# Two-part values product, a later load of x and queued weight splits in a hybrid attention layer

## The chip, the cores and the metric

One core of a Trainium2 chip runs one launch of the kernel. The metric is the device time of that launch in microseconds (us). Five engines work in parallel, each through its own queue in order: PE (TensorE, matrix products), DVE (VectorE), ACT (ScalarE), POOL (GpSimd) and SP (SyncE, which here only issues DMAs). PEld is PE's loading of the stationary operand, which overlaps the products.

## The reference

One decoder layer over 256 tokens of width 1024. One projection feeds three token mixers; their outputs are gated, merged and normalised, and a feed-forward part with a second gate follows.

```python
proj = x @ w_in[i]
o_a = dsa_mixer(...)      # 6 heads, one k and v for all, the 64 best keys by an index
o_b = dilated_mixer(...)  # 3 groups x 4 slots, merged over the groups: 4 value products
o_c = moba_mixer(...)     # 6 heads, 256 keys
gates = jax.nn.sigmoid(x @ w_gate[i]).reshape(bsz, s_len, N_BRANCH, D_MODEL)
merged = (gates[:, :, 0] * (o_a @ w_br_a[i]) + gates[:, :, 1] * (o_b @ w_br_b[i])
          + gates[:, :, 2] * (o_c @ w_br_c[i]))
x = layer_norm(ALPHA * x + merged @ w_out[i], ln1_g[i], ln1_b[i])
h = jnp.square(jax.nn.relu(x @ w_up[i])) @ w_down[i]
ple = jax.nn.sigmoid(x @ w_ple_gate[i]) * (p[i] @ w_ple[i])
x = layer_norm(ALPHA * x + h + ple, ln2_g[i], ln2_b[i])
```

## The kernel before

Every float32 product is made from two-part operands: a high part `hi`, the value rounded to the type F32R, and a low part `lo`, what the rounding left, and three products hi·hi, hi·lo and lo·hi (`prod`, L131 to L134). A product of 128x128 stationary values with a moving block of 256 or 512 columns is called a pass here.

**Weights.** `Weights` (L50 to L90) streams the weights in units of up to 128x1024. For each unit SP loads it into one of five `raw` buffers (L71), ACT makes `hi` (L75) and DVE, or DVE and POOL together for the first 58 units, makes `lo` (L79), into five pairs of buffers. The next load into a `raw` buffer waits until its `lo` is made. `get` asks for the splits four units ahead; whatever stands in `W.after` at that moment is an instruction behind which the split is queued on that instruction's engine. Every engine works in the order in which a scheduler put the program at build time.

**Heads (to about 193 us).** For each of 16 heads, `head` or `slots` (L338 to L373) turns logits into probabilities P, laid out as 384 columns: 128 for the queries 0 to 127 (keys 0 to 127) and 256 for the queries 128 to 255 (all keys). `attend` (L307) transposes P in three 128x128 blocks into a PSUM bank (L312 to L314), makes `hi` (ACT, L315) and `lo` (DVE, L316) in 512-wide tiles `pth` and `ptl`, whose first 128 columns were set to zero once by POOL (L194), and makes four passes of 256 columns (L319 to L322) with the stationary `V[:, j, vh]`. The 128 columns of `V` hold the high part of a value head in the first 64 and the low part in the last 64, so the output's rows 0 to 63 and 64 to 127 must be added: ACT copies the lower half to `ov` (L324) and DVE adds it to the upper one (L325). There is one PSUM bank for the transposes (b3) and one for the outputs (b4). `pair_out` splits a pair of heads into `op` (ACT L328, DVE L329). Between the heads PE is filled with passes of the gate products ("g") and of the branch products ("c", `fill` L233).

**Merges (about 196 to 206 us).** Four calls of `merge` (L559) each make 18 passes over `op[:, 0..2]`, gate them on DVE (L568, L569) and split two tiles `m` (ACT L572, DVE L573). `outp` (L577) multiplies these tiles with the eight units of `w_out` into four banks b0 to b3, 96 passes of 512 columns: units 0 to 3 by `step`, units 4 to 7, whose parts lie in `hT`, by `finish` (L545), which ends first the two banks of the tokens 0 to 127 (b = 0: b0 and b1), then those of b = 1 (b3 and b2).

**First layer norm (about 226 to 241 us).** `ln1` (L621) adds ALPHA·x, which the ACT queue loads into `PL` (L596, 1 MB), takes statistics (L605 to L613, one of them on POOL, L612), norms with the rows `rows1` (L593, 1 MB, ACT queue), transposes the result (L632) and splits it into `x1` (ACT L634, DVE L635). The product of p with `w_ple` (24 passes, L649) doesn't depend on it; its results go into `PL` too (L651). The gate product `pg` (96 passes) then takes `x1`.

**After it** come the products with `w_up` (L681, L683) to about 349 us, those with `w_down` (with sums that save products) to about 428 us, and the second layer norm.

Of the kernel before, what the change touches and what calls it, by code (L numbers as in the profile page):

```python
# [11 lines left out]
F32 = mybir.dt.float32  # L12
F32R = mybir.dt.float32r
ALU = mybir.AluOpType
# [6 lines left out]
S = 256  # L21
# [72 lines left out]
def hybrid_layer(ctx: ExitStack, tc: tile.TileContext, x0, xn, pT, wqk, wva, wvb, wg, wbc, wba,  # L94
                 wout, wup, wdq, wdn, wpg, wple, lnrow, rel, mask, out):
    nc = tc.nc
    pe, act, dve, pool = nc.tensor, nc.scalar, nc.vector, nc.gpsimd
# [8 lines left out]
    W = Weights(tc, raw, part)  # L106
# [9 lines left out]
    ident = keep.tile([128, 128], F32, name="ident")  # L116
# [71 lines left out]
        return t  # L188


    pth = [p1.tile([128, 512], F32R, name=f"pth{i}") for i in range(2)]
    ptl = [p1.tile([128, 512], F32R, name=f"ptl{i}") for i in range(2)]
    for t in pth + ptl:
        pool.memset(t[:, 0:128].bitcast(F32), 0.0)  # L194

    idx = p1.tile([128, 384], F32, name="idx")
    am = p1.tile([128, 384], F32, name="am")
# [107 lines left out]
    n_pt = [0]  # L305

    def attend(P, vh, o, h):  # L307

        hi, lo = pth[n_pt[0] % 2], ptl[n_pt[0] % 2]
        n_pt[0] += 1  # L310
        t = next(ps_t)
        pe.transpose(t[:, 0:128], P[:, 256:384], ident)  # L312
        pe.transpose(t[:, 128:256], P[:, 0:128], ident)
        pe.transpose(t[:, 256:384], P[:, 128:256], ident)  # L314
        act.copy(hi[:, 128:512], t[:, 0:384])  # L315
        dve.tensor_tensor(lo[:, 128:512], t[:, 0:384], hi[:, 128:512].bitcast(F32),  # L316
                          op=ALU.subtract)
        v = next(ps_v)
        pe.matmul(v[:, 0:S], lhsT=V[:, 0, vh], rhs=hi[:, 256:512], start=True, stop=False)  # L319
        pe.matmul(v[:, 0:S], lhsT=V[:, 0, vh], rhs=lo[:, 256:512], start=False, stop=False)  # L320
        pe.matmul(v[:, 0:S], lhsT=V[:, 1, vh], rhs=hi[:, 0:256], start=False, stop=False)  # L321
        pe.matmul(v[:, 0:S], lhsT=V[:, 1, vh], rhs=lo[:, 0:256], start=False, stop=True)  # L322
        x = wk2.tile([64, S], F32, name="ov", tag="ov")
        act.copy(x, v[64:128, 0:S])  # L324
        dve.tensor_tensor(o[64 * h:64 * h + 64], v[0:64, 0:S], x, op=ALU.add)  # L325

    def pair_out(o, kt):
        act.copy(op[:, kt, 0], o)  # L328
# [224 lines left out]
                    done(b, c, self.acc[b][c])  # L553

    T2 = (slice(0, 128), slice(128, 256))
    mt = []


    def merge(p):  # L559
        hi, lo = W.get(u_ba[p][0])  # L560
        ps = mmbank(512).rearrange("p (f s) -> p f s", f=2)
        for f in range(2):
            for k in range(3):
                c = slice((3 * f + k) * 128, (3 * f + k + 1) * 128)
                prod(ps[:, f], (hi[:, c], lo[:, c]), (op[:, k, 0], op[:, k, 1]), k == 0, k == 2)
        g6 = G[:, 6 * p:6 * p + 6].rearrange("p (f i) s -> p f i s", f=2)
        g = g6[:, :, 0]
        dve.scalar_tensor_tensor(g, g, 1.0, ps, op0=ALU.add, op1=ALU.mult)  # L568
        dve.tensor_tensor(g, g, g6[:, :, 1], op=ALU.add)  # L569
        for f in range(2):  # L570
            m = qpool.tile([128, 2, S], F32R, name="q", tag="q")
            act.mul(m[:, 0], g[:, f], 0.5)  # L572
            dve.scalar_tensor_tensor(m[:, 1], g[:, f], 0.5, m[:, 0].bitcast(F32), op0=ALU.mult,  # L573
                                     op1=ALU.subtract)
            mt.append(m)

    outp = Wide(u_out, lambda k, b: (mt[k][:, 0, T2[b]], mt[k][:, 1, T2[b]]))  # L577
    for p in range(4):
        merge(p)
    for k in range(4):  # L580
        outp.step(k)
    mid.close()


# [7 lines left out]
    def row_load(t, i):  # L592
        act.dma_start(t, lnrow[i:i + 2].rearrange("r d -> (r d)").partition_broadcast(128)  # L593
                      .rearrange("p (r d) -> p r d", r=2))

    act.dma_start(PL, xn)  # L596
    row_load(rows1, 0)

    st = {}

# [329 lines left out]
```

## Time and profile before

| what | before |
|---|---|
| device time, median of 3 runs | 442.63 us (442.06 to 443.55) |
| device time of the profiled execution | 442.14 us |
| span of the profile | 440.4 us |
| PE, DVE, ACT, POOL busy | 97%, 77%, 61%, 23% |
| PE's share of the chain that ended last | 93% |
| bytes moved | 84.29 MB, mean 191 GB/s |
| granted TensorE clock, share of full speed | 0.997 |

The span is what the profile covers; 1.74 us of the profiled execution's time lie around it. The profile's "chain that ended last" is found by going back from the last instruction, at each step to what released it or to the instruction before it on its engine. A row of the timeline gives the start, the duration, the engine, the line and the tiles (out <- in), and in brackets the idle time before it with what ended it. Matmuls are pipelined: the duration shown is longer than the distance to the next one, so what a pass costs PE is read from the distance between starts.

### The profile page before, as it was taken

What the parts mean: (1) busy time and instruction counts of PE and PEld (TensorE: products, weight loads), DVE (VectorE), ACT (ScalarE), POOL (GpSimd) and SP (SyncE); (2) the same over time, 40 slices, a digit from 0 to 9 for tenths busy, and PEclk for the clock granted to TensorE, in tenths of its full rate; (3) what the DMA queues carried; (4) which work ended last, traced back from release to release, by engine and by line L of the source; (5) the groups of instructions that cost most, each with busy time, mean ns of one, the idle gap of its engine ahead of it and who ended that gap; (6) DMA issues with size and microseconds to landing.
All of it is one profiled execution on the core that took longest, in us unless ns stands there. A gap on an engine that the chain in (4) does not pass through costs nothing.

```text
span 440.4 us, 7719 instructions
## 1 busy us (share of the span) xinstructions
PE 429.0 (97%) x2837; PEld 388.7 (88%) x2837; DVE 337.4 (77%) x602; ACT 269.8 (61%) x487; POOL 101.7 (23%) x98
## 2 busy tenths in 40 slices
PE   8999999999999999998999999999999999999992
PEld 8999999999999999998886888888888888888882
DVE  4978977475664588768958779999888978588956
ACT  6775375584787766855605567888877765456500
POOL 3564355397543644400001000000000000000001
PEclk9999999999999999999999999999999999999998
DMA  8896765448544345467860866668655364655502
GB/s 282 316 313 219 238 187 176 158 129 314 161 148 130 124 152 164 140 193 288 258 265 0 281 221 185 187 193 284 198 183 183 105 212 144 250 151 204 226 0 96
DMA packets 27113, 84.29 MB, mean 191 GB/s; under 512 B 2820, under 2 KB 6828, under 8 KB 26692
## 3 DMA queue, kind: packets, MB, share of 16 engines
q1 hardware_dynamic: 25872, 79.54, 55.5%
q10 hardware_dynamic: 1140, 4.19, 2.6%
q8 instruction: 22, 0.36, 0.3%
q14 instruction: 15, 0.12, 0.1%
q0 software_dynamic: 64, 0.07, 0.1%
HBM read 81.90 MB, written 1.90 MB: 190 GB/s over the span
## 4 chain that ended last, share of the span: by engine, by line
PE 93%; DVE 2%; DMA 2%; issue 2%; ACT 1%; POOL 0%; POOLq 0%; DVEq 0%; ACTq 0%
PE mm L134 39%; PE b L134 23%; PE mm L681 13%; PE mm L683 7%; PE b L273 3%; PE b L407 3%; DMA raw<-in_wout_dram 2%; PE b L129 1%; PE b L319 1%; ACT whi L75 0%; PE b L320 0%; PE b L322 0%; PE b L321 0%; PE b L312 0%; PE b L314 0%
## 5 line engine op out<-in xcount | busy, mean ns | idle before, releaser
L79 DVE TENSOR_TENSOR wlo<-raw,whi 128x1024 fp32r<-128x1024 f32 (+5 forms) x147 | 157.4, 1085 | 42.1 <-ACT whi L75 38.6
L75 ACT CAST whi<-raw 128x1024 fp32r<-128x1024 f32 (+3 forms) x147 | 147.8, 1011 | 57.4 <-PE mm L134 17.2
L79 POOL TENSOR_TENSOR wlo<-raw,whi 128x384 fp32r<-128x384 f32 (+3 forms) x58 | 77.3, 1342 | 81.8 <-ACT whi L75 67.2
L134 PE MATMUL mm<-xl,whi 128*128 128x256 f32 x336 | 95.5, 284 | 0.0
L134 PE MATMUL mm<-xh,whi 128*128 128x256 f32 x336 | 95.1, 283 | 0.0
L134 PE MATMUL mm<-xh,wlo 128*128 128x256 f32 x336 | 95.0, 283 | 0.0
L134 PEld LDWEIGHTS mm<-xl,whi 128*128 128x128 f32 x336 | 63.3, 188 | 0.9
L681 PE MATMUL mm<-x,whi 128*128 128x512 f32 x256 | 64.1, 392 | 0.0
L134 PEld LDWEIGHTS mm<-xh,wlo 128*128 128x128 f32 x336 | 63.3, 188 | 0.6
L134 PEld LDWEIGHTS mm<-xh,whi 128*128 128x128 f32 x336 | 63.3, 188 | 0.2
L612 POOL TENSOR_TENSOR rs<-rs,half 128x1 f32<-128x1 f32 x4 | 4.1, 1028 | 246.0 <-DVE rs L611 246.0
L134 PE MATMUL b<-whi,hT 128*128 128x512 f32 (+1 forms) x176 | 55.0, 379 | 0.0
L681 PEld LDWEIGHTS mm<-x,whi 128*128 128x128 f32 x256 | 46.1, 189 | 8.3
L134 PEld LDWEIGHTS b<-whi,hT 128*128 128x128 f32 x176 | 32.7, 188 | 6.2
L683 PEld LDWEIGHTS mm<-x,wlo 128*128 128x128 f32 x256 | 34.9, 190 | 2.5
L683 PE MATMUL mm<-x,wlo 128*128 128x256 f32 x256 | 35.7, 282 | 0.0
L134 PE MATMUL b<-wlo,hT 128*128 128x512 f32 (+1 forms) x88 | 33.4, 380 | 0.0
L686 DVE TENSOR_REDUCE r<-mm 128x256 f32<-128x512 f32 x32 | 22.0, 687 | 5.9 <-PE mm L683 5.9
L134 PE MATMUL mm<-op,whi 128*128 128x256 f32 x128 | 23.3, 281 | 0.0
L742 DVE TENSOR_TENSOR raw<-raw 128x1024 f32<-128x1024 f32 x12 | 14.7, 1222 | 9.2 <-DMA raw<-in_wdq_dram 9.2
L134 PE MATMUL b<-whi,x 128*128 128x512 f32 x64 | 20.5, 396 | 0.3 <-ACT x L634 0.3
L240 ACT ACTIVATE G<-mm 128x256 f32<-128x256 f32 x24 | 9.2, 382 | 18.3 <-PE mm L134 18.2
(171 smaller groups left out, 712.2 us busy)
## 6 DMA issues: line engine op xcount, KB each, us to landing
raw<-in_wup_dram SPq DMA_DIRECT2D x32, 512.0 KB
raw<-in_wg_dram SPq DMA_DIRECT2D x24, 512.0 KB
raw<-in_wdn_dram SPq DMA_DIRECT2D x20, 512.0 KB
raw<-in_wqk_dram SPq DMA_DIRECT2D x18, 512.0 KB
raw<-in_wdq_dram SPq DMA_DIRECT2D x12, 512.0 KB
raw<-in_wout_dram SPq DMA_DIRECT2D x8, 512.0 KB
raw<-in_wpg_dram SPq DMA_DIRECT2D x8, 512.0 KB
T<-tabd SPq DMA_DIRECT2D x24, 128.0 KB
```

What stands on the lines that cost most here:

```text
L75: nc.scalar.copy(hi, r)
L79: e.tensor_tensor(lo[:, c], r[:, c], hi[:, c].bitcast(F32), op=ALU.subtract)
L129: pe.transpose(t[:, 0:128], ident, ident)
L134: pe.matmul(ps, lhsT=a[x], rhs=b[y], start=first and i == 0, stop=last and i == 2)
L240: act.activation(G[:, n_g[0]], ps, AF.Tanh, scale=0.5)
L273: m = pe.matmul(ss[h][:, QC[b]], lhsT=q[d, x, c], rhs=k[d, y, 0:128 * (b + 1)], start=i == 0, stop=i == 2)
L319: pe.matmul(v[:, 0:S], lhsT=V[:, 0, vh], rhs=hi[:, 256:512], start=True, stop=False)
L407: pe.matmul(first[f], lhsT=w[:, k, 128 * f:128 * f + 128], rhs=x[:, k], start=k == i == 0, stop=k == KT - 1 and i == 2)
L681: pe.matmul(ps, lhsT=hi[:, cs[k]], rhs=x1[:, :, k], start=k == 0, stop=False)
L683: pe.matmul(ps[:, :, 0], lhsT=lo[:, cs[k]], rhs=x1[:, :, k, 0], start=False, stop=k == KT - 1)
L686: dve.tensor_reduce(r, ps.rearrange("p b a t -> p b t a"), axis=AX.X, op=ALU.add)
L742: dve.tensor_tensor(t[n], t[x], t[y], op=ALU.subtract)
```

## The change

Three edits. The line numbers of the changed kernel are up to five lower.

- `attend` keeps both parts of the transposed probabilities in one tile `pt` of 128 x 2 x 384, in the order of P. The first product takes the columns 0 to 255 of both parts at once (512 moving columns: the keys 0 to 127 for all queries), the second the last 128 columns of both parts (2 x 128: the keys 128 to 255 for the queries 128 to 255), added onto a part of the same bank. The zero blocks and the four memsets are gone. The output is now 128 x 2 x 256; ACT copies 64x512 in place of 64x256, DVE adds 64x512, and one more DVE instruction adds the two halves.
- While the merges are traced, each split requested after the first merge is queued behind the last `mul` (ACT) and the last low part (DVE) of the first merge, and each one requested after the second merge behind those of the second.
- The loads of x into `PL` and of `rows1` are queued on ACT behind `muls[5]`, the last `mul` of the third merge.

```diff
-    pth = [p1.tile([128, 512], F32R, name=f"pth{i}") for i in range(2)]
-    ptl = [p1.tile([128, 512], F32R, name=f"ptl{i}") for i in range(2)]
-    for t in pth + ptl:
-        pool.memset(t[:, 0:128].bitcast(F32), 0.0)
+    pts = [p1.tile([128, 2, 384], F32R, name=f"pt{i}") for i in range(2)]
...
     def attend(P, vh, o, h):
-        hi, lo = pth[n_pt[0] % 2], ptl[n_pt[0] % 2]
+        pt = pts[n_pt[0] % 2]
         n_pt[0] += 1
         t = next(ps_t)
-        pe.transpose(t[:, 0:128], P[:, 256:384], ident)
-        pe.transpose(t[:, 128:256], P[:, 0:128], ident)
-        pe.transpose(t[:, 256:384], P[:, 128:256], ident)
-        act.copy(hi[:, 128:512], t[:, 0:384])
-        dve.tensor_tensor(lo[:, 128:512], t[:, 0:384], hi[:, 128:512].bitcast(F32),
-                          op=ALU.subtract)
-        v = next(ps_v)
-        pe.matmul(v[:, 0:S], lhsT=V[:, 0, vh], rhs=hi[:, 256:512], start=True, stop=False)
-        pe.matmul(v[:, 0:S], lhsT=V[:, 0, vh], rhs=lo[:, 256:512], start=False, stop=False)
-        pe.matmul(v[:, 0:S], lhsT=V[:, 1, vh], rhs=hi[:, 0:256], start=False, stop=False)
-        pe.matmul(v[:, 0:S], lhsT=V[:, 1, vh], rhs=lo[:, 0:256], start=False, stop=True)
-        x = wk2.tile([64, S], F32, name="ov", tag="ov")
-        act.copy(x, v[64:128, 0:S])
-        dve.tensor_tensor(o[64 * h:64 * h + 64], v[0:64, 0:S], x, op=ALU.add)
+        for c in range(3):
+            pe.transpose(t[:, 128 * c:128 * c + 128], P[:, 128 * c:128 * c + 128], ident)
+        act.copy(pt[:, 0], t[:, 0:384])
+        dve.tensor_tensor(pt[:, 1], t[:, 0:384], pt[:, 0].bitcast(F32), op=ALU.subtract)
+        v = next(ps_v).rearrange("p (a s) -> p a s", a=2)
+        pe.matmul(v, lhsT=V[:, 0, vh], rhs=pt[:, :, 0:256], start=True, stop=False)
+        pe.matmul(v[:, :, 128:256], lhsT=V[:, 1, vh], rhs=pt[:, :, 256:384], start=False,
+                  stop=True)
+        x = wk2.tile([64, 2, S], F32, name="ov", tag="ov")
+        act.copy(x, v[64:128])
+        dve.tensor_tensor(x, v[0:64], x, op=ALU.add)
+        dve.tensor_tensor(o[64 * h:64 * h + 64], x[:, 0], x[:, 1], op=ALU.add)
...
         for f in range(2):
             m = qpool.tile([128, 2, S], F32R, name="q", tag="q")
-            act.mul(m[:, 0], g[:, f], 0.5)
-            dve.scalar_tensor_tensor(m[:, 1], g[:, f], 0.5, m[:, 0].bitcast(F32), op0=ALU.mult,
-                                     op1=ALU.subtract)
+            muls.append(act.mul(m[:, 0], g[:, f], 0.5).ins)
+            low = dve.scalar_tensor_tensor(m[:, 1], g[:, f], 0.5, m[:, 0].bitcast(F32),
+                                           op0=ALU.mult, op1=ALU.subtract)
             mt.append(m)
+        if p < 2:
+            W.after = (muls[-1], low.ins)
...
     for k in range(4):
         outp.step(k)
+    W.after = ()
     mid.close()
...
-    act.dma_start(PL, xn)
-    row_load(rows1, 0)
+    with tc.issue_after(muls[5]):
+        act.dma_start(PL, xn)
+        row_load(rows1, 0)
```

The scheduler makes a new order from this. Three pieces of it follow.

On ACT, at the merges, before: the casts of the units of `w_out` (`whi`, and `hT` for the units from 4 on), the split of the last pair of heads (`op`), the load of x (`in_xn_dram`) and the first merge's muls (L572).

```order
L75 CAST whi_2923<-raw_2921 128x768
L328 CAST op_135<-o_2625 128x256
L75 CAST whi_2964<-raw_2962 128x1024
L596 DMA PL_2956<-in_xn_dram 128x2048
L75 CAST whi_2997<-raw_2995 128x1024
L75 CAST hT_2955<-raw_3094 128x1024
L75 CAST whi_3030<-raw_3028 128x1024
L572 ACTIVATE q_2989<-G_114 128x256
L572 ACTIVATE q_2992<-G_114 128x256
```

And after the change, from the same cast of the last unit of the branch weights (128x768):

```order
L75 CAST whi_2901<-raw_2899 128x768
L75 CAST whi_2942<-raw_2940 128x1024
L323 CAST op_129<-o_2605 128x256
L567 ACTIVATE q_2967<-G_114 128x256
L567 ACTIVATE q_2970<-G_114 128x256
L75 CAST whi_2975<-raw_2973 128x1024
L567 ACTIVATE q_3000<-G_114 128x256
L567 ACTIVATE q_3003<-G_114 128x256
L75 CAST whi_3008<-raw_3006 128x1024
L75 CAST whi_3041<-raw_3039 128x1024
L75 CAST hT_2933<-raw_3072 128x1024
L75 CAST hT_2933<-raw_3088 128x1024
```

The first merge's muls now stand behind one cast of `w_out` in place of four, the cast of unit 4 (`hT`) no longer stands ahead of that of unit 2, the split of the last pair of heads has moved behind the cast of unit 0, and the load of x has left this place: it stands behind the third merge's muls, which follow these rows.

On DVE at the same place, before: the low parts of the units (L79), of `op` (L329), and the gating of the merges (L568, L569).

```order
L79 TENSOR_TENSOR wlo_2924<-raw_2921,whi_2923 128x768
L329 TENSOR_TENSOR op_135<-o_2625,op_135 128x256
L254 TENSOR_TENSOR G_114<-G_114 128x256
L253 SCALAR_TENSOR_TENSOR G_114<-G_114,mm_2927 128x512
L79 TENSOR_TENSOR wlo_2965<-raw_2962,whi_2964 128x1024
L254 TENSOR_TENSOR G_114<-G_114 128x256
L568 SCALAR_TENSOR_TENSOR G_114<-G_114,mm_2968 128x2x256
L79 TENSOR_TENSOR wlo_2998<-raw_2995,whi_2997 128x1024
L569 TENSOR_TENSOR G_114<-G_114 128x2x256
L568 SCALAR_TENSOR_TENSOR G_114<-G_114,mm_3001 128x2x256
L79 TENSOR_TENSOR hT_2955<-raw_3094,hT_2955 128x1024
L79 TENSOR_TENSOR wlo_3031<-raw_3028,whi_3030 128x1024
```

And after, from the low part of `w_out`'s unit 0 on:

```order
L79 TENSOR_TENSOR wlo_2943<-raw_2940,whi_2942 128x1024
L324 TENSOR_TENSOR op_129<-o_2605,op_129 128x256
L251 TENSOR_TENSOR G_114<-G_114 128x256
L563 SCALAR_TENSOR_TENSOR G_114<-G_114,mm_2946 128x2x256
L564 TENSOR_TENSOR G_114<-G_114 128x2x256
L563 SCALAR_TENSOR_TENSOR G_114<-G_114,mm_2979 128x2x256
L568 SCALAR_TENSOR_TENSOR q_2967<-G_114,q_2967 128x256
L564 TENSOR_TENSOR G_114<-G_114 128x2x256
L568 SCALAR_TENSOR_TENSOR q_2970<-G_114,q_2970 128x256
L563 SCALAR_TENSOR_TENSOR G_114<-G_114,mm_3012 128x2x256
L79 TENSOR_TENSOR wlo_2976<-raw_2973,whi_2975 128x1024
L568 SCALAR_TENSOR_TENSOR q_3000<-G_114,q_3000 128x256
```

The gating and the low parts of the first two merges now come before the low part of unit 1, and the low part of `op` stands behind that of unit 0.

On PE, in the output product, before: banks b0 to b3 are the output product's, `mm` tiles with `ph` and `pl` are the product of p with `w_ple`.

```order
L134 MATMUL b2_2961<-hT_2955,q_3055 128x512 x2
L134 MATMUL mm_3301<-wlo_3176,ph_82 128x512
L134 MATMUL mm_3301<-whi_3175,pl_83 128x512
L134 MATMUL mm_3301<-whi_3181,ph_82 128x512
L134 MATMUL mm_3309<-wlo_3176,ph_82 128x512
L134 MATMUL mm_3309<-whi_3175,pl_83 128x512
L134 MATMUL mm_3309<-whi_3181,ph_82 128x512
L134 MATMUL mm_3317<-wlo_3176,ph_82 128x512
L134 MATMUL mm_3317<-whi_3175,pl_83 128x512
L134 MATMUL mm_3317<-whi_3181,ph_82 128x512
L134 MATMUL b0_2958<-hT_2955,q_3055 128x512
```

And after, at the first transposes of the normed x (L631):

```order
L134 MATMUL mm_3295<-whi_3153,pl_83 128x512
L134 MATMUL mm_3295<-whi_3159,ph_82 128x512
L134 MATMUL mm_3295<-wlo_3160,ph_82 128x512
L134 MATMUL mm_3295<-whi_3159,pl_83 128x512
L631 MATMUL b4_3211<-ident_75,Y_3146 128x128 x4
L134 MATMUL mm_3303<-whi_3153,ph_82 128x512
L134 MATMUL mm_3303<-wlo_3154,ph_82 128x512
L134 MATMUL mm_3303<-whi_3153,pl_83 128x512
L134 MATMUL mm_3303<-whi_3159,ph_82 128x512
L134 MATMUL mm_3303<-wlo_3160,ph_82 128x512
L134 MATMUL mm_3303<-whi_3159,pl_83 128x512
L631 MATMUL b0_3220<-ident_75,Y_3146 128x128 x4
```

Before, 12 of the 24 passes with `w_ple` lay inside the output product and 12 between its end and the first transposes. Now none lies inside; 18 stand between its end and the first transposes, and 6 between the first and the second four transposes. On SP the order of the loads is the same.

More of the change, by code (lines that the diff above doesn't have):

```diff
@@ L555, in hybrid_layer @@
     T2 = (slice(0, 128), slice(128, 256))
-    mt = []
+    mt, muls = [], []
     def merge(p):
```

## The prediction

> **What bounds the kernel now.** I read the page first, then busy time by window, then the chain.
>
> ```profile
> span 440.4 us, 7719 instructions
> ...
> PE 429.0 (97%) x2837; PEld 388.7 (88%) x2837; DVE 337.4 (77%) x602; ACT 269.8 (61%) x487; POOL 101.7 (23%) x98
> ...
> PE 93%; DVE 2%; DMA 2%; issue 2%; ACT 1%; POOL 0%; POOLq 0%; DVEq 0%; ACTq 0%
> ```
>
> PE bounds it: 93% of the chain that ended last. So only two things shorten the time: fewer columns on PE, and fewer gaps between its passes. The windows say where gaps can be (start:end, length, then busy us and count of PE, PEld, DVE, ACT, POOL; clock, DMA share, GB/s).
>
> ```profile
> 65.00:195.00 130.00, 130.00 (x1108) 127.44 (x1108) 82.20 (x196) 88.34 (x203) 66.88 (x57) 1.00 0.52 166
> 195.00:240.00 45.00, 43.49 (x237) 36.14 (x235) 37.02 (x59) 19.43 (x29) 2.00 (x2) 1.00 0.61 211
> ```
>
> From 65 to 195 us, where the 16 heads lie, PE never idles; DVE has 48 of 130 us free. From 195 to 240 us, the merges and the first norm, PE loses time. The durations of PE rows overlap, so I take a pass from the chain, which has starts one after the other:
>
> ```profile
> 188.56 0.12 PE b L320
> 188.68 0.12 PE b L321
> 188.80 0.12 PE b L322
> ...
> 189.03 0.11 PE b L313
> ...
> 189.25 2.96 PE mm L134 x25
> ...
> 222.25 9.07 PE b L134 x40
> ...
> 259.59 1.81 PE mm L681 x8
> 261.40 0.95 PE mm L683 x8
> ```
>
> 256 columns cost 2.96/25 = 0.118 us, 512 columns 9.07/40 = 0.227 us, a transpose 0.11 us. L683 moves 2 x 128 columns with steps on both sides, and also costs 0.95/8 = 0.119 us.
>
> **The values product.** Per head four passes of 256 columns, 4 x 0.118 = 0.474 us, become one of 512 (0.227; L681's 1.81/8 gives 0.226) and one of 2 x 128 (0.119): 0.346 us. That saves 0.128 us x 16 heads = **2.05 us**, all on a PE without gaps. The cost stands on ACT and DVE.
>
> ```profile
> L324 ACT COPY ov<-b 64x256 f32<-64x256 f32 x16 | 5.9, 370 | 11.2 <-PE b L322 11.0
> L651 ACT ACTIVATE PL<-mm 128x512 f32<-128x512 f32 x4 | 2.2, 599 | 12.1 <-PE mm L134 12.1
> L325 DVE TENSOR_TENSOR o<-b,ov 64x256 f32<-64x256 f32 x16 | 6.6, 415 | 4.0 <-ACT ov L324 3.8
> L253 DVE SCALAR_TENSOR_TENSOR G<-G,mm 128x512 f32<-128x512 f32 x8 | 5.4, 683 | 4.7 <-PE mm L134 4.7
> 169.90 1.24 DVE L254 TENSOR_TENSOR G<-G 128x256 f32<-128x256 f32 x1
> 185.22 0.41 DVE L254 TENSOR_TENSOR G<-G 128x256 f32<-128x256 f32 x1
> 169.20 2.51 POOL L79 TENSOR_TENSOR wlo<-raw,whi 128x384 fp32r<-128x384 f32 x2 [2.62 <-ACT whi L75]
> ```
>
> The copy of 512 columns takes 0.60 us as L651 does, 0.23 more than now; the addition of 512 columns 0.68, as L253, 0.27 more. The new addition has both inputs in SBUF, as L254 has: 0.41 us alone, 1.24 where POOL ran beside it. So DVE gains 16 x (0.27 + 0.41 to 1.24) = 11 to 24 us in a stretch with 48 free, ACT 3.7 us. In the new order of PE, 24 passes or more lie between a head's transposes and its values product: 24 x 0.118 = 2.8 us for one cast and one subtraction, and as many at least between an output and the next that needs its bank, for 0.60 + 0.68 = 1.3 us and what is queued ahead. The cover suffices on average; some heads may wait. I take +0.3 us, bounds 0 and 16 x 0.49 (both longer reads of the bank bare) = +7.8. The memsets cost nothing now either: POOL's next split comes at 14.8 us, long after.
>
> [...]
>
> **The merges.** What ends PE's gap:
>
> ```profile
> 196.74 0.34 ACTq L596 DMA_DIRECT2D PL<-in_xn_dram  x1
> ...
> 203.90 1.05 ACT L75 CAST hT<-raw 128x1024 fp32r<-128x1024 f32 x1 [3.21 <-DMA raw<-in_wout_dram]
> 204.86 1.04 ACT L75 CAST whi<-raw 128x1024 fp32r<-128x1024 f32 x1
> 205.80 0.72 ACT L572 ACTIVATE q<-G 128x256 fp32r<-128x256 f32 x2
> ...
> 204.88 0.28 PE L134 MATMUL mm<-op,wlo 128*128 128x256 f32 x1
> 206.27 0.50 PE L134 MATMUL b<-whi,q 128*128 128x512 f32 x1 [1.11 <-ACT q L572]
> ...
> 197.10 6.72 DMA raw<-in_wout_dram
> ...
> 206.27 7.83 PE b L134 x32
> ```
>
> ACT stood 3.21 us before the cast of unit 4, whose 512 KB needed 6.72 us beside x's 1 MB, issued 0.36 us earlier; the first merge's mul stood behind it. PE's last merge pass starts at 204.88 and ends 0.12 later; the output product starts at 206.27: 1.27 us lost. Its first 32 passes take 7.83 where 32 x 0.227 = 7.26: 0.57 more, together 1.84.
>
> After the change the first mul stands behind the cast of unit 0 alone. Now what takes the wait's place: the split of the last `op` pair has moved behind that unit.
>
> ```profile
> 195.71 0.40 ACT L328 CAST op<-o 128x256 fp32r<-128x256 f32 x1
> 196.72 1.05 ACT L75 CAST whi<-raw 128x1024 fp32r<-128x1024 f32 x1 [0.61 <-issue]
> ...
> 198.26 1.22 DVE L79 TENSOR_TENSOR wlo<-raw,whi 128x1024 fp32r<-128x1024 f32 x1
> 199.39 0.42 DVE L254 TENSOR_TENSOR G<-G 128x256 f32<-128x256 f32 x1
> ```
>
> On before's clock: the merges are 72 passes that end at 205.00, so they begin at 205.00 - 72 x 0.118 = 196.5. Unit 0's cast starts at 196.72 and will not start sooner, since it needs a buffer that the last pass ahead of the merges frees. The cast of `op` follows 0.95 us later (casts start that far apart at 203.90 and 204.86) and ends at 196.72 + 0.95 + 0.40 = 198.1; PE wants it after 12 passes, at 197.9: 0.15 us. The low part of `op` follows unit 0's, at 197.8 + 1.13 (the step from 198.26 to 199.39), and is done 0.42 later, at 199.3; PE wants it after 21 passes and that wait, at 199.1: 0.2 us. Then the first merge's products end at about 200.7; DVE's two gating steps (0.68 each, as L253) and the mul (0.36) give `q` at 202.5, its low part by 203.1, and PE asks at 205.4. Counted on along DVE's new order in the same way, the units 1 to 3 have their low parts at about 206, 209 and 210.5; PE asks for them after 16, 28 and 40 passes, at 209, 211.7 and 214.4. So 0.35 remains plus 0.1 for a start, and **1.4 us** of 1.84 go. Bounds: 0 and 1.84.
>
> The load of x goes behind the third merge's muls. After the first two muls (0.72, at 202.2) ACT has five casts (0.95 each) and four more muls (2 x 0.72): 202.2 + 0.72 + 4.75 + 1.44 = 209.1. At the 7 us that unit 4 took beside it, x lands near 216. It is read when b0's product ends, 76 passes or 17.2 us after the merges' end: 222. It now runs beside unit 7 of `w_out` and the loads of `w_ple`; at 7 us for these too (asked for at about 208 to 210) they land by 217, and PE wants unit 7 some 67 passes after the merges' end, at 220, and `w_ple` after 96, at 227. The rows' load follows on ACT a few casts later, near 216, and is wanted near 226; SP issues the same loads in the same order.
>
> **The first norm.** PE's passes with `w_ple` are the cover:
>
> ```profile
> 231.32 2.81 PE mm L134 x12
> ...
> 235.26 0.69 DVE x L635
> ...
> 237.25 0.68 DVE x L635
> ...
> 239.98 19.61 PE b L134 x84
> ...
> 231.94 0.68 DVE L622 SCALAR_TENSOR_TENSOR Y<-PL,b 128x512 f32<-128x512 f32 x1
> 232.53 1.41 DVE L619 SCALAR_TENSOR_TENSOR Y<-Y,rs,rows 128x512 f32<-128x512 f32 x2
> 233.86 0.69 DVE L605 BATCH_NORM_STATS2 st<-Y 128x6 f32<-128x512 f32 x1
> ...
> 237.85 1.41 DVE L619 SCALAR_TENSOR_TENSOR Y<-Y,rs,rows 128x512 f32<-128x512 f32 x2
> ```
>
> The 12 passes after the output product end at 231.32 + 12 x 0.227 = 234.04. From there to 239.98 PE issues 16 transposes and 12 passes, 16 x 0.11 + 12 x 0.227 = 4.48 us, in 5.94: 1.46 lost, because the second half's norm is ready only at 237.85 + 1.41 = 239.3, 8 us after the output product's end (222.25 + 9.07 = 231.3). In the new order two subtractions (L635, 0.68 each) and DVE's wait for ACT's `x` leave that chain. What DVE still does after the output product's end, by its new order and these rows, a step of 512 columns at 0.6 to 0.7: the rest of one half's statistics 0.9, one step of the first half's norm 0.7, the sum 0.6, the other step 0.7, statistics 0.9, and the second half's four steps 2.7 = 6.5 us. PE's cover is 26 passes and 8 transposes: 26 x 0.227 + 0.88 = 6.8 us. It just suffices; I take 0.2 us left, so **1.26 us** go, bounds 0 and 1.46. The 12 passes that leave the output product uncover nothing: its units are split 2 us or more ahead (above).
>
> **Sum.** -2.05 - 1.4 - 1.26 + 0.3 = -4.4 us. The profiled execution took 442.14 (span 440.4 and 1.74 around it): 442.14 - 4.4 = **437.7 us**. The median, 442.63, is 0.5 above that execution, within the runs' spread; from it the sum would give 438.2. The stages after 260 us have no gap to give and move as a whole.
>
> **Rivals.**
> - *The norm's cover fails* (its slack is 0.4 us, and DVE's splits of the gate weights now end about when b0 is done): 1.26 us stay, 439.0.
> - *The merges wait for `op` as long as they did for `q`*: 1.4 us stay, 439.1; with the norm's too, 440.4. Against it: `op` is late by 0.35 us only. That the edits don't do what they say comes to this as well; the rows of the order speak against it.
> - *Slower: DVE holds up the heads.* Each values product waits for the output bank. From 0.29 us a head (4.7/16) the gain is gone; with 0.49 us bare, 16 x 0.49 = 7.8: 442.14 - 4.7 + 7.8 = 445.2. For it: 1.24 us beside POOL, which is busy half of this stretch. Against it: 2.8 us of cover, DVE 63% busy before and 72 to 82% after.
> [...]
> - *x lands late for the norm*: from 6 us of further delay, nearly as long again as the load; then each further us costs one: 437.7 + 1 or 2.
>
> **Chances.** Forecast (436.3 to 438.7) 0.66; norm's cover 0.10; merges, alone or with the norm, 0.09; heads 0.08; steps 0.03; others 0.04. A measurement of this kernel tells about 0.3%, 1.3 us, from no change, so faster means under 441.3: 0.86; the same 0.06, from mixtures with waits at the heads; slower 0.08. The range goes from every gap closed with no new wait (442.14 - 2.05 - 1.84 - 1.46 = 436.8, less 0.5 for the spread) to both gaps kept (440.4, and 0.3): 436.3 to 440.7.
>
> **What would show it.** In the new profile: value products of 0.227 and 0.119 us and PE without a gap from 65 to 193 us (values, heads); the output product's first pass within 0.3 us of the last merge pass, ACT's wait of 3.21 us before `hT` gone, x's load issued after the third merge's muls; at most 0.5 us lost between the output product and the second half's transposes. Wrong it would be if idle time on PE ends by DVE `ov` or ACT `pt` among the heads, by `op` at the merges, or by DVE `Y` at the norm.

## The result and the profile after

| | before | after |
|---|---|---|
| median of 6 runs each, same chip | 442.5 us (441.84 to 443.55) | 439.41 us (438.36 to 440.45) |
| ratio after/before, 95% interval | | 0.9929 (0.991 to 0.9949) |
| profiled execution, its span | 442.14, 440.4 | 438.36, 436.3 |
| DVE busy, ACT busy | 337.4, 269.8 | 346.4, 273.2 |

The changed kernel is faster, by 3.1 us of the median; 437.7 was forecast, 436.3 to 440.7 the range. The page of after:

```profile
PE 425.7 (98%) x2805; PEld 386.0 (88%) x2805; DVE 346.4 (79%) x618; ACT 273.2 (63%) x487; POOL 102.4 (23%) x94
...
PE 95%; DVE 2%; issue 1%; POOL 0%; POOLq 0%; ACT 0%; DVEq 0%
```

PE's share of the chain rose from 93 to 95%. What is left is in the view of PE's waits from 65 to 245 us, the heads, the merges and the norm (what waited, for what: us in total, times, longest). Before:

```profile
PE b L134 <- ACT q L572: 1.1, 1, 1.1
PE b L134 <- ACT x L634: 0.3, 1, 0.3
```

And after:

```profile
PE mm L134 <- DVE G L250: 0.5, 1, 0.5
PE mm L134 <- DVE op L324: 0.4, 1, 0.4
```

The wait for `q` and that of the norm are gone, and two new ones have come: one among the heads (`G`), one in the merges (`op`). This view counts only idle PE, 0.5 and 0.4 us; by starts, as worked out below, 0.70 us are lost among the heads and 1.18 in the merges, where the passes behind the wait also start further apart (0.22 to 0.29 us in place of 0.117).

The chain of after at the heads, near 155 us:

```profile
154.76 0.23 PE b L314
155.00 0.12 PE b L315
155.12 0.33 PE b L310 x3
155.44 0.49 PE mm L134 x4
155.93 0.02 issue
155.95 0.70 DVE G L250
156.65 0.04 issue
156.69 0.39 PE mm L134
```

The values product takes 0.23 + 0.12 us, as forecast. But behind it come the last passes of two branch products (`mm`), and the next gate product finds no free `mm` bank until DVE has read out the first of them (L250). PE's last pass before that starts at 155.87, the next at 156.69: 0.82 for a pass of 0.118, **0.70 us lost**. DVE had been idle until that bank's last pass:

```profile
155.95 0.69 DVE L250 SCALAR_TENSOR_TENSOR G<-G,mm 128x512 f32<-128x512 f32 x1 [1.21 <-PE mm L134]
```

In the merges, the first pass and the first pass of the output product; first after, then a kernel that differs in the values product alone (second experiment: both other edits, four passes a head as before):

```profile
195.25 0.28 PE L134 MATMUL mm<-op,whi 128*128 128x256 f32 x1
...
204.83 0.39 PE L134 MATMUL b<-whi,q 128*128 128x512 f32 x1
```

```profile
196.79 0.40 PE L134 MATMUL mm<-op,whi 128*128 128x256 f32 x2
...
205.19 0.40 PE L134 MATMUL b<-whi,q 128*128 128x512 f32 x1
```

PE comes to the merges 196.79 - 195.25 = 1.54 us sooner. Of this 0.68 are scatter at the start (the projections' first pass starts at 16.75 and 17.43), so 0.86 come from the heads. At the output product 205.19 - 204.83 = **0.36** are left: the 72 merge passes take 9.58 us here and 8.40, or 0.117 each, in the other, **1.18 us lost**. Why, DVE and ACT of after show in the timeline:

```profile
193.60 0.68 DVE L319 TENSOR_TENSOR ov<-b,ov 64x512 f32<-64x512 f32 x1
194.20 0.67 DVE L250 SCALAR_TENSOR_TENSOR G<-G,mm 128x512 f32<-128x512 f32 x1
194.79 0.94 DVE L79 TENSOR_TENSOR wlo<-raw,whi 128x768 fp32r<-128x768 f32 x1
195.77 0.42 DVE L320 TENSOR_TENSOR o<-ov 64x256 f32<-64x256 f32 x1
...
197.16 1.22 DVE L79 TENSOR_TENSOR wlo<-raw,whi 128x1024 fp32r<-128x1024 f32 x1
198.30 0.42 DVE L324 TENSOR_TENSOR op<-o,op 128x256 fp32r<-128x256 f32 x1
```

```profile
195.38 1.05 ACT L75 CAST whi<-raw 128x1024 fp32r<-128x1024 f32 x1 [0.91 <-PE mm L134]
196.33 0.40 ACT L323 CAST op<-o 128x256 fp32r<-128x256 f32 x1
```

The last head's first addition ends at 194.28; the second one (L320) stands behind a `G` and a split and ends at 196.19; `op` then stands behind unit 0 on both engines, and its low part is there at 198.72, 3.5 us after the first merge pass. In the other kernel it is there at 197.61, 0.8 us after it.

Behind the merges nothing is lost. The chain of after, from the output product's end to the gate product:

```profile
226.80 4.08 PE mm L134 x18
230.88 0.44 PE b L631 x4
231.32 1.38 PE mm L134 x6
232.70 0.44 PE b L631 x4
```

PE goes through the first norm without a wait. ACT's wait of 3.21 us before unit 4 is gone, and the load of x is issued at 206.69, behind the third merge's muls.

### The profile page after: what moved, and what is told of

Read it like the earlier page. It is cut to its first block, busy times and chain, and to the rows that moved or that the text cites. A ratio compares the mean times of both kernels' runs of the same rounds, so it can differ in the third digit from the quotient of the medians.

```text
span 436.3 us, 7650 instructions
## 1 busy us (share of the span) xinstructions
PE 425.7 (98%) x2805; PEld 386.0 (88%) x2805; DVE 346.4 (79%) x618; ACT 273.2 (63%) x487; POOL 102.4 (23%) x94
## 4 chain that ended last, share of the span: by engine, by line
PE 95%; DVE 2%; issue 1%; POOL 0%; POOLq 0%; ACT 0%; DVEq 0%
PE mm L134 41%; PE b L134 24%; PE mm L680 13%; PE mm L682 7%; PE b L270 3%; PE b L402 3%; PE b L310 1%; PE b L314 1%; PE b L129 1%; DVE wlo L79 1%; DVE G L250 0%; PE b L315 0%; PE b L631 0%; POOLq L925 0%; POOL rs L611 0%
## 5 line engine op out<-in xcount | busy, mean ns | idle before, releaser
L79 DVE TENSOR_TENSOR wlo<-raw,whi 128x1024 fp32r<-128x1024 f32 (+5 forms) x147 | 157.9, 1088 | 38.7 <-ACT whi L75 36.0
L79 POOL TENSOR_TENSOR wlo<-raw,whi 128x384 fp32r<-128x384 f32 (+3 forms) x58 | 78.4, 1358 | 81.2 <-ACT whi L75 73.6
L134 PE MATMUL mm<-op,whi 128*128 128x256 f32 x128 | 24.6, 285 | 0.4 <-DVE op L324 0.4
L134 PEld LDWEIGHTS mm<-op,whi 128*128 128x128 f32 x128 | 19.8, 188 | 1.4 <-DVE op L324 0.6
```

The costliest lines, as they stand in the source:

```text
L79: e.tensor_tensor(lo[:, c], r[:, c], hi[:, c].bitcast(F32), op=ALU.subtract)
L134: pe.matmul(ps, lhsT=a[x], rhs=b[y], start=first and i == 0, stop=last and i == 2)
```

## Experiments

All times are medians of 6 to 12 runs, ratios are to runs of the kernel before on the same chip, with 95% intervals. "Lost" is time between starts of PE's passes beyond the passes' own length. An edit makes the scheduler order every engine anew, so each kernel's profile was read for its own waits.

### One edit or two alone

`e1_values`: the first edit alone. `e2_queue_and_load`: the second and third. `e3_queue_only`: the second (`W.after`). `e4_load_only`: the third. The diffs are those parts of the change.

> The kernel before with the first edit alone (values product in two passes); splits and the load of x as before. Theory (the terms add): 16 x 0.128 = 2.05 us go from PE between 65 and 195 us, 0.3 to 0.9 us come back as waits among the heads, and the gaps before the output product (1.84 us) and at the first norm (1.46) stay: 440.2 to 441.0 by the profiled execution of before (442.14), ratio 0.995 to 0.998. Rival 1 (the values product gives nothing: what PE saves is lost to waits for the output bank): 442 to 443, with PE's lost time among the heads 2 us or more. Rival 2 (the values product is the whole gain): 439.0 to 439.5.

Measured 443.63 us, ratio 1.0014 (0.9992 to 1.0036): nothing is gained. My theory that the terms add fell; rival 1 is nearest (its range ends 0.6 below the time), but has the place wrong. PE's waits from 195 to 245 us in that kernel, and PE's busy time by window (start:end, length, busy us and count of PE, PEld, DVE, ACT, POOL; clock, DMA share, GB/s):

```profile
PE b L134 <- DVE q L568: 2.3, 1, 2.3
PE b L134 <- ACT q L567: 0.5, 1, 0.5
PE mm L134 <- DVE op L324: 0.4, 1, 0.4
```

```profile
208.00:212.00 4.00, 1.70 (x8) 1.10 (x7) 4.00 (x6) 2.79 (x5) 0.00 (x0) 1.00 0.88 286
212.00:216.00 4.00, 4.00 (x12) 3.12 (x12) 4.00 (x7) 2.65 (x4) 0.00 (x0) 0.57 0.68 238
216.00:220.00 4.00, 4.00 (x19) 3.31 (x18) 4.00 (x6) 1.68 (x3) 0.00 (x0) 1.00 0.94 343
```

The late pair delays the merges, their gating on DVE falls behind splits of `w_out`, and the output product waits for `q` in two places. The span of this execution is 443.4 us: what the passes save and 3 us more are lost, most of it here and part of that at a granted clock of 0.57 from 212 to 216 us (last section). This execution took 445.48 us, 1.85 above the median, so the median doesn't hold all of that loss.

> The changed kernel without its first edit: splits queued behind the merges, x loaded after the third merge's muls, the values product in four passes as before. Theory (the terms add): the values products keep 2.05 us, nothing is lost among the heads, the gap before the output product and most of the norm's go (1.1 to 1.8 and 1.3 to 1.5): 438.9 to 439.8, ratio 0.992 to 0.995. Rival (the values product is the whole gain): 442 and a ratio of 0.999 to 1.001, with PE's gaps at the merges or the norm still above 2.5 us in sum.

Measured 438.42 us, ratio 0.9887 (0.9863 to 0.9911): without its first edit the changed kernel is no slower. That is 0.5 below the theory's range: these two edits hold the whole gain. From 65 to 245 us PE waits for nothing; the 72 merge passes take 0.117 us each, as shown above.

> The kernel before with the second edit alone (splits queued behind the merges); x is loaded early, as before. Theory: the first mul no longer stands behind the cast of unit 4, so the gap of 1.27 us and the slow first 32 passes go although x still runs beside unit 4: 1.1 to 1.8 us less at the merges, and the norm gains as with both edits since its order of passes is nearly the same: 439.0 to 440.2. Rival (the early load of x is what delays, whatever the queue): unit 4 lands late still and the output product waits for it: 440.7 to 442, with PE waiting for whi of a later unit.

Measured 439.51 us, ratio 0.9909 (0.9886 to 0.9933), as the theory had it: the queue alone carries nearly the whole gain, with x loaded as early as before. One wait is left, 0.3 us at the norm.

> The kernel before with the third edit alone (x loaded behind the third merge's muls); the splits run ahead as before. Theory: ACT's wait before the cast of unit 4 shrinks from 3.21 us to 1 or less, but the first mul still stands behind five casts; half of the 1.84 us go, and the norm keeps its loss, since its order of passes is that of before: 440.7 to 441.7. Rival (the load is the whole cause at the merges): 1.84 us or more go, 440.3 or less. Rival 2 (a later x is late for the norm): PE waits over 2 us at the norm for DVE Y behind PL: above 442.

Measured 441.81 us, ratio 0.9964 (0.9949 to 0.9979), 0.1 above the theory's range. PE's waits:

```profile
PE b L134 <- DVE q L573: 0.8, 1, 0.8
PE b L134 <- ACT x L636: 0.5, 2, 0.3
```

Unit 4 comes sooner, but the merges' gating still stands behind the splits: the wait moves from `q`'s high part to its low part, and the norm keeps its own. By starts the output product begins 1.08 us sooner behind the first merge pass than before, but its first 32 passes then take 0.86 longer. So the queue is the cause at the merges, and the load adds little once the queue is right (e2 against e3; their intervals overlap).

### What the values product costs

New theory: the edit saves the time of its passes, but lengthens the way from a head's output to `op`, and gives the time back where PE waits for a pair. The next four ran on one chip.

> The changed kernel once more, on the same chip as the next three. Theory now (the values edit saves 2.05 us of passes and gives nearly all of it back in waits): 438.3 to 440.5, ratio 0.991 to 0.995, and a second profile with the same two waits, 0.5 to 0.8 us of a gate pass behind G near 156 us and 0.5 to 0.8 for op in the merges; PE loses 1 us more in sum than without the values edit. Rival (the waits were those of one execution): PE loses under 0.9 us between 100 and 240 us, and the median is 1.2 us or more below that of the kernel without the values edit.

Measured 439.18 us, ratio 0.9907 (0.9879 to 0.9935). Both waits are there again, 0.71 us lost near 156 us, and the merge passes take 9.58 us as in the first profile.

> The changed kernel without the values edit, again, beside it on one chip. Theory (that edit is worth nothing here): 437.9 to 439.5, ratio 0.987 to 0.991, level with the changed kernel or up to 1 us below it. Rival (the two medians came from different chips, and the edit gives what its passes save): 1.2 to 2 us above the changed kernel.

Measured 439.66 us, ratio 0.9915 (0.9887 to 0.9943): 0.2 above the theory's range and 0.5 above the changed kernel, short of the 1.2 to 2 of the rival. This kernel's two medians differ by 1.2 us, as the runs of one kernel scatter by 1 to 2 us here (its second profile lost 0.6 us to a wait at the norm that the first didn't have). Over 12 runs each, the medians are 439.30 for the changed kernel and 438.98 without the first edit: that edit is worth nothing that these runs can tell.

`e7_op_first`: unit 0's split queued behind the last pair's.

```diff
+        opi[0] = act.copy(op[:, kt, 0], o).ins
+        opi[1] = dve.tensor_tensor(op[:, kt, 1], o, op[:, kt, 0].bitcast(F32), op=ALU.subtract).ins
...
+    W.after = tuple(opi)
     for p in range(4):
         merge(p)
```

> The changed kernel with the split of the first unit of w_out queued behind the split of the last op pair, on ACT and on DVE. Theory: the wait for op (0.55 + 0.17 us) goes and nothing comes in its place, since that unit's split still ends 2 us ahead of the output product: 0.5 to 0.7 us below the changed kernel, 437.7 to 439.3, ratio 0.989 to 0.993. Rival (the wait moves on: the merges' own G or the first mul is late next): within 0.2 us of the changed kernel, with a new wait of 0.4 us or more before the output product.

Measured 438.85 us, ratio 0.9901 (0.9868 to 0.9933), 0.33 below the changed kernel, less than the theory's 0.5 to 0.7. In its profile the merge passes take 8.99 us in place of 9.58: half of the loss goes. The second addition still stands behind two instructions of DVE.

`e8_lean_values`: four passes added up in place, none longer than needed, on top of queue and load.

```diff
+        pe.matmul(v[:, 0:S], lhsT=V[:, 0, vh], rhs=pt[:, 0, 0:256], start=True, stop=False)
+        pe.matmul(v[:, 0:S], lhsT=V[:, 0, vh], rhs=pt[:, 1, 0:256], start=False, stop=False)
+        pe.matmul(v[:, 128:S], lhsT=V[:, 1, vh], rhs=pt[:, 0, 256:384], start=False, stop=False)
+        pe.matmul(v[:, 128:S], lhsT=V[:, 1, vh], rhs=pt[:, 1, 256:384], start=False, stop=True)
```

> Queue and load as changed, and a values product of four passes without the zero block: both parts by 256 columns, then both parts by 128, all added up in one place, so ACT and DVE work as before the change. Theory (it is the longer copy and the additions that cost the gain, and a pass of 128 columns takes half of 0.118 us): 16 x 2 x 0.059 = 1.9 us below the kernel without the values edit, 436.2 to 437.6, ratio 0.983 to 0.987. Rival (a pass of 128 columns takes as long as one of 256, as the transposes of 128 columns take 0.11 us): level with the kernel without the values edit, 438 to 439.5.

Measured 438.7 us, ratio 0.99 (0.9871 to 0.9929), above the theory's range and within the rival's (438 to 439.5). PE and PEld at one head:

```profile
150.80 0.28 PE L315 MATMUL b<-pt,V 128*128 128x256 f32 x1
150.81 0.19 PEld L316 LDWEIGHTS b<-pt,V 128*128 128x128 f32 x1
150.92 0.22 PE L316 MATMUL b<-pt,V 128*128 128x128 f32 x1
150.92 0.19 PEld L317 LDWEIGHTS b<-pt,V 128*128 128x128 f32 x1
150.98 0.28 PE L317 MATMUL b<-pt,V 128*128 128x128 f32 x1
151.03 0.30 PEld L134 LDWEIGHTS mm<-op,whi 128*128 128x128 f32 x2
151.09 0.33 PE L134 MATMUL mm<-op,whi 128*128 128x256 f32 x1
151.38 0.28 PE L134 MATMUL mm<-op,wlo 128*128 128x256 f32 x1
```

The first pass of 128 columns costs 150.98 - 150.92 = 0.06 us, the second 0.11: loads of the stationary operand start 0.11 us apart (150.81, 150.92, 151.03), and no pass here starts before its own load does. But the passes behind them give the time back: from 150.80 to 151.38 five passes start in 0.58 us, 0.116 each, and passes of 256 columns take 0.117. Over the whole stretch, from the projections' first pass to the first merge pass, it is 179.25 us here and 179.36 before: the shorter passes save next to nothing, and the rival holds. In the wait view PE waits for nothing from 65 to 245 us, since ACT and DVE do what they did before. The median lies 1.0 below that of e6, but in the profiles the difference of the two lies elsewhere: here the projections begin 0.84 us sooner, and e6 has its wait at the norm.

### The additions

`e9_one_addition` writes `o` from the first half alone; `e10_pool_adds` has the second addition on POOL.

```diff
-        dve.tensor_tensor(x, v[0:64], x, op=ALU.add)
-        dve.tensor_tensor(o[64 * h:64 * h + 64], x[:, 0], x[:, 1], op=ALU.add)
+        dve.tensor_tensor(o[64 * h:64 * h + 64], v[0:64, 0], x[:, 0], op=ALU.add)  # e9
...
-        dve.tensor_tensor(o[64 * h:64 * h + 64], x[:, 0], x[:, 1], op=ALU.add)
+        pool.tensor_tensor(o[64 * h:64 * h + 64], x[:, 0], x[:, 1], op=ALU.add)    # e10
```

> The changed kernel without the second addition of the output's halves: the low part's half of a head's output is left out, so that DVE has 16 instructions less and each pair is ready about 0.9 us sooner (0.42 and what stands ahead of it). The four memsets at the start are put back, onto pt, to see whether the 0.3 us that this kernel takes more around its span belong to them. Theory: in its order of PE too the last four branch passes stand directly ahead of the gate product that needs the bank, so 0.6 to 0.75 us stay lost there near 155 us, while the wait for op in the merges goes (its cast stands ahead of unit 0's again): 0.4 to 0.8 us below the changed kernel, 438.2 to 438.9. Rival (DVE's second addition itself holds PE up): both waits go, 1.2 to 1.6 us below it. Around the span: 1.8 us if the memsets matter, 2.1 if not.

Measured 438.01 us, ratio 0.9882 (0.9856 to 0.9908), 0.2 below the theory's range. Both statements of the theory hold in the profile: the merge passes take 8.40 us, the whole wait for `op` gone, and 0.71 us stay lost near 156 us although DVE has an addition less. That wait is one of order, not of DVE's load. Near 113 us this kernel has a new one: transposes wait for ACT, 0.44 us lost.

> The changed kernel with the second addition on POOL in place of DVE. In its order the cast of op stands ahead of unit 0's, and the last six branch passes directly ahead of the gate product. Theory: the wait for op goes (below 0.3 us left), the one near 155 us stays (0.6 to 0.75): 0.4 to 0.7 us below the changed kernel, 438.4 to 439. Rival (POOL is no cheaper: both inputs are in SBUF, as those of the addition that took 1.24 us beside POOL): DVE's splits or branch sums beside the 16 additions become slower by 0.4 us or more each, new waits of 0.5 us and more among the heads, level with the changed kernel or above it.

Measured 437.34 us, ratio 0.9873 (0.985 to 0.9896): 1.1 us better than the theory's range, and 1.8 to 2.1 below the changed kernel's medians, taken at another time. The only wait of PE left in the view is that for `G`, 0.5 us. The group of additions on POOL:

```profile
L320 POOL TENSOR_TENSOR o<-ov 64x256 f32<-64x256 f32 x16 | 14.1, 879 | 21.7 <-DVE ov L319 16.1 <-PE mm L134 4.4 <-DVE r L328 1.0
```

An addition takes 0.88 us here against 0.46 on DVE, but it waits in no queue: the output product begins at 203.41, 1.42 us sooner than after the change (204.83), of which 1.18 come from the merges (8.40 us again). DVE's splits beside it became slower, 953 ns on average in place of 899, which nothing waits for.

`e11_combined`: this, the four memsets back, and the second branch product's last passes behind the first's. `e12_transposes_behind`: also the next head's transposes behind them.

```diff
+                    with ExitStack() as order:
+                        if f == 1 and k == k1 - 1 and i:
+                            order.enter_context(tc.issue_after(c_end[0]))
+                        c_end[1] = prod(ps[:, i], (hi[:, c], lo[:, c]),
+                                        (op[:, k, 0], op[:, k, 1]), k == k0, k == k1 - 1)
+            c_end[0] = c_end[1]
...
+            if n_pt[0] == 12:                                  # e12
+                order.enter_context(tc.issue_after(c_end[0]))
             for c in range(3):
                 pe.transpose(t[:, 128 * c:128 * c + 128], P[:, 128 * c:128 * c + 128], ident)
```

> The changed kernel with the second addition on POOL, the four memsets put back, and the last three passes of the second branch product queued behind those of the first, so that the first one's bank is read out 0.35 us sooner. Theory: of the 0.7 us near 155 us half goes (0.3 to 0.4 left), the time around the span is 1.8 us in place of 2.1, and the rest is as with the addition on POOL (437.34): 436.5 to 437.2, ratio 0.985 to 0.987. Rival (the bank that the gate product waits for is that of the second branch product, or of neither): 0.65 us or more stay lost near 155 us, and only 0.3 us are gained: 437.0 to 437.4.

Measured 437.14 us, ratio 0.9852 (0.9822 to 0.9883). The time lies in the range. The mechanism held and my size did not: 0.59 us are lost near 156 us in place of 0.71 (PE's passes start at 156.19 and 156.90). The first bank's last pass had been the fourth of six and is now the third, so it is read one pass, 0.12 us, sooner, not 0.35. This is the fastest kernel of the study, not to be told from e10.

> The combined kernel, and the next head's three transposes queued behind the last pass of the first branch product (they stood ahead of it). Theory (the gate product waits for DVE's reading of the first branch product's bank, 0.69 us and the steps around it, and each pass of PE between the two covers its own length): 0.33 us of the 0.59 go, 0.2 to 0.3 are left lost near 156 us, and nothing else changes: 436.5 to 437.2, ratio 0.984 to 0.987, not to be told from the combined kernel by its time. Rival (it waits for another bank or for DVE's own queue): 0.5 us or more stay lost there.

Measured 437.77 us, ratio 0.9873 (0.9843 to 0.9904), 0.6 above the theory's range. Near 156 us 0.25 are lost (156.38 and 156.75), as the theory said: the three transposes put between DVE's reading and the gate product, 0.11 us each, cover 0.34 of the 0.59. But the other half of the expectation fell. PE's only wait in the view is now a new one, and DVE shows whose:

```profile
PE b L325 <- DVE pt L323: 0.7, 1, 0.7
```

```profile
161.16 1.91 DVE L259 TENSOR_TENSOR G<-G 128x256 f32<-128x256 f32 x1
162.99 0.54 DVE L323 TENSOR_TENSOR pt<-b,pt 128x384 fp32r<-128x384 f32 x1
```

The later transposes push the low part of `pt` behind a split and a branch sum on DVE, and the values product waits for it.

## Why the prediction was right, and where it was wrong

The forecast of 437.7 is 1.7 below the median and 0.7 below the profiled execution; sign and range were right. The sum came out in part by luck, through stages that were off in opposite directions. The table has the starts of the same passes in both profiles; the difference is what the stage that ends there became shorter by.

| stage ends with the start of | before | after | difference | forecast |
|---|---|---|---|---|
| first pass of the projections | 17.24 | 16.75 | -0.49 | 0 |
| first merge pass (heads) | 196.60 | 195.25 | -0.86 | -2.05 + 0.3 |
| first pass of the output product (merges) | 206.27 | 204.83 | -0.09 | -1.4, with the next row |
| pass behind its first 32 | 213.93 | 212.13 | -0.36 | |
| first pass with `w_up` (norm) | 259.42 | 255.66 | -1.96 | -1.26 |
| PE's last pass | 431.90 | 428.14 | 0 | 0 |
| end of the span | 440.4 | 436.3 | -0.3 | 0 |
| around the span (length) | 1.74 | 2.06 | +0.3 | 0 |
| sum | | | -3.8 | -4.4 |

The heads and the merges gave 1.3 us where 3.15 were forecast; the norm gave 0.7 more than forecast, and 0.5 came from the start. The start is scatter: the projections' first pass starts at 16.69 to 17.53 us in the fourteen profiles, at 16.75 and 17.07 in the two of the changed kernel. The profile of after also happens to be the lowest of its six runs, which is most of what separates it from the median.

- **Values product.** The two passes cost 0.351 us a head where L681 and L683 had given 0.346, in place of 0.471: 1.9 us in all. The steps of the second one, to which the chances give 0.03, did not slow it: 0.12 us for 2 x 128 columns, where 256 in a row take 0.118. What I had wrong was the worth of the term: alone it gave nothing (e1), with the others nothing that can be told (e2, e6).
- **Heads.** I asked whether the output bank comes free in time, and it does: no wait on `ov`. Of the 1.9 us that the passes save, 1.0 are lost in this profile and 0.8 in that of e5. 0.70 of them come from another bank. The pair is ready later, the scheduler put its branch passes behind the values product and the transposes, and nothing is left between them and the gate product to cover 0.69 us of DVE. The rival of slow heads named DVE's load; DVE stood idle before that reading, and e9 shows that the wait stays with an addition less. Another 0.2 us are lost near 113 us, where transposes wait for ACT; the profile of e5 doesn't have this.
- **Merges.** This step failed. The wait for `q` went fully, as e2 and e3 show (8.40 us for the merge passes, 9.67 before). But "0.35 remains" was worked out on before's clock, with the merges beginning at 196.5, while my own first term brings PE there sooner, at 195.25, and not the pair: `op` hangs on the last head's output, whose way to `op` had become longer by a longer copy, a longer addition and a second addition. I priced that way as throughput and never followed it to `op` for the last pair. It cost 1.18 us where I had 0.35 and 0.1 for a start: PE stands 0.13 us for the high part and 0.55 for the low one, and the passes behind them start 0.22 to 0.29 us apart (196.78, 197.00, 197.30, 197.52; 198.77, 198.99), which is 0.5 more. e7, which changes the order alone, takes half of that away. e9 and e10 shorten the way and take all of it away; in their orders the cast of `op` also stands ahead of unit 0's again. The size to be gained was misread too: the product's first 32 passes take 7.66 us by their starts before and 7.30 after, so 0.36 were lost there and not 0.57. The chain's piece of 7.83 runs to 214.10, while the next pass starts at 213.93. So 1.63 us could go, not 1.84.
- **Norm.** The cover sufficed, with 0.4 us of slack forecast, and more went than the 1.46 I had seen. Three passes behind 239.98 took 0.34, 0.39 and 0.33 us in place of 0.227, which I hadn't counted; where the last 0.1 lay stays open. In one later profile, of e6, 0.6 us came back, so the slack is about used up.
- **The load of x** was in time as forecast, and worth little beside the queue (e3).
- **The slower rival** (DVE holds up the heads, 445.2) did not happen; a time like it was met by the profiled execution of e1 (445.48), through the merges and not the heads.

## What to carry to other kernels

A saving on the bounding engine ahead of a point where it waits for another only lengthens that wait, unless the other's way is shortened too (here 1.9 us saved by the passes, 1.0 lost among the heads and 1.18 in the merges); follow the new instructions from the product to who reads their result last, not only to the buffer that they free. When work moves off the bound engine onto one with half its time free, ask where its new instructions stand in that engine's queue: an addition of 0.42 us, queued behind a split, and the order that the scheduler made with it set off a loss of 1.2, and the same addition on POOL, slower there at 0.88 us but idle ahead of it (21.7 us before the 16 additions), set off none there. Run each edit of a change alone: here one of three carried the gain, and moving that addition brought 1.4 us more by the starts of the passes, and about 2 by the medians (437.34).

## What the hardware showed that I had not expected

- **A lower clock behind a gap.** In e1 the output product stood for 2.5 us, from 208.79 to 211.25, and the windows above show a granted clock of 0.57 from 212 to 216 us and 1.00 at either side; passes of 512 columns took 0.43 us in place of 0.227 (rows below), and the 12 passes from 211.25 on took 4.54 us where 12 x 0.227 = 2.72. What set the clock back, and how long a gap that takes, is not shown: before, behind 1.27 us lost at the same place, the clock is 1.00 in every window from 205 to 216 us. The kernel before scatters upward, 441.7 to 446.0 us in the 66 runs beside the experiments, its 23 runs from 443.9 up at a mean granted clock of 0.989 to 0.993 and the 43 others at 0.992 to 0.997; none of those was profiled, so whether such a stretch lies behind that is not shown either.

```profile
208.56 0.39 PE L134 MATMUL b<-wlo,q 128*128 128x512 f32 x1
211.25 1.56 PE L134 MATMUL b<-whi,q 128*128 128x512 f32 x5 [2.30 <-DVE q L568]
212.60 0.63 PE L134 MATMUL b<-wlo,q 128*128 128x512 f32 x1
213.03 0.63 PE L134 MATMUL b<-whi,q 128*128 128x512 f32 x1
```

- **Passes of 128 columns saved next to nothing (e8).** Loads of the stationary operand started 0.11 us apart there. A pass of 128 columns started the next one 0.06 us on, but the two passes from 151.09 on took 0.29 us, so the five came to 0.116 each, as much as passes of 256 columns. The zero block of the kernel before therefore cost next to nothing (179.36 us over the stretch with it, 179.25 without), and the edit saves time on PE by having two passes in place of four (0.351 us a head in place of 0.471).
- **DVE beside POOL.** The branch sum of e12, 0.41 us alone (185.22 in the profile of before), took 1.91 from 161.16 on, while POOL went through an addition (1.06) and a split (1.00).
- **0.3 us outside the span.** The time around the span is 2.0 to 2.3 us in every run of after, e1, e5, e7 and e8, and 1.7 to 1.9 in every run of the others. With the memsets back it is 1.8 (e9), but also without them where POOL has the additions (e10); what sets it stays open. In the profile of after the span also ends 0.3 us closer behind PE's last pass (8.2 in place of 8.5), so the two cancel there.
